# Token-major projections paired to 512 columns, two heads' products issued side by side, some weight splits made by GpSimd DMA

## The chip, the cores and the metric

The kernel runs on one NeuronCore of one Trainium2 chip. The metric is the device time of one execution in microseconds; it is given as the median of a few runs.

## The reference

Two decoder layers run over 256 tokens of width 1024 in float32. Each layer has a mixer with four groups of 256 columns and a convolutional FFN:

```python
proj = einsum('bsd,de->bse', rms_norm(x, norm_mix[i]), w_in[i])
qa, ka, va, qb, kb, vb, c_val, c_gate, qm = split(proj, 9 sections of 256)
o_a = moba_attention(rope(norm(qa)), rope(norm(ka)), va)       # 4 heads of 64, causal
o_b = dilated_attention(rope(norm(qb)), rope(norm(kb)), vb)    # 4 heads of 64, causal
o_c = silu(layer_norm(depthwise_conv31(c_val * sigmoid(c_gate)))) @ w_conv_out
km, vm = split(rms_norm(mem) @ w_mem_kv[i])                    # memory of 256 rows
o_m = softmax(norm(qm) @ norm(km).T * scale) @ vm              # 4 heads of 64, no mask
x = x + group_rms_norm(concat(o_a, o_b, o_c, o_m)) @ w_out[i]
gate, val = split(depthwise_conv3(rms_norm(x) @ w_up[i]))      # width 2 x 2816
x = x + (silu(gate) * val) @ w_down[i]
```

## The kernel before

**Split products.** Most products are made in fp32r, with both operands split into a high and a low part. An activation has the tiles `Hh` and `Hl`. A weight unit of 128x2048 floats (1 MB) is staged in an `st` slot by a DMA on SyncE's queue; ACT copies it, rounded, into a `wh` slot and DVE writes the difference `st - wh` into a `wl` slot, 1024 columns at a time (`get`, `split`). One product is then three matmuls: `wh` with `Hh`, `wl` with `Hh`, `wh` with `Hl`. There are 4 `st`, 3 `wh` and 3 `wl` slots, and `INORDER` makes them, and the two PSUM banks `pj`, be handed out in the order of the units. A few products are plain fp32: layer 0's first section (the gate `cg`, from the tile `whole`, which sits in an `st` slot) and the output products of groups 1 and 3 (`gy` with `st`).

**Sections.** A section is one of the nine 256-column parts of `w_in`, or `km` or `vm`; its unit holds all 8 chunks of 128 rows. The two convolution sections are channel-major (`proj`), the other nine token-major (`proj_tok`): the stationary operand is a 128-token block of `Hh` or `Hl`, the moving one 256 columns of `wh` or `wl`, so a section is 2 token blocks x 8 chunks x 3 = 48 matmuls of 256 columns. After it `head_norm` makes squares on ACT, head by head with an accumulator, then the rope and the scaling on DVE, four transposes on PE and a copy on ACT. `ORDER` gives the sections of a layer in the order of their units; the memory sections of layer 1 are made in layer 0's FFN.

**Attention.** For two chunks of two heads each, `attention` records per head: two score products (64 contraction rows, PSUM tag `sc`), softmax on DVE and ACT, transposes, and a copy; then per head two products with V (64 output rows, tile `o`). Three `sc` banks serve both scores and transposes.

**Order.** Nothing is issued directly: operations are recorded on logical tiles with an estimated duration, a list scheduler (`schedule`) picks for each engine the operation that can start first by these estimates, and `emit` issues the result. Each engine then runs its own list strictly in order and waits on semaphores. Issues of DMAs stand in SyncE's list in the same way.

Of the kernel before, what the change touches and what calls it, by code (L numbers as in the profile page):

```python
# [10 lines left out]
F32 = mybir.dt.float32  # L11
# [24 lines left out]
PASSES = ((1,0),(3,),(2,))  # L36
CO_AT = 1
# [28 lines left out]
def unit_order():  # L66
    names = []
    for l in range(DEPTH):
        for s in ORDER[l]:
            names += [(l, s)] if s != "mem" else [(l, "mem"), (l, "km"), (l, "vm")]  # L70
# [4 lines left out]
        for i in range(NPAIR):  # L75
            names.append((l, f"up{i}"))
            if i == MEM_AT and l + 1 < DEPTH:
                names += [(l + 1, "mem"), (l + 1, "km"), (l + 1, "vm")]
# [21 lines left out]
def pack_weights(i):  # L100
    parts = []
    for l, n in UNITS:
# [5 lines left out]
        elif n in ("km", "vm"):  # L108
            s = ("km", "vm").index(n)
            parts.append(kpack(i["w_mem_kv"][l][:, s * GW:(s + 1) * GW]))  # L110
# [83 lines left out]
class View:  # L194
# [21 lines left out]
    def heads(self):  # L216
        """[P, 2, 256] as [P, 2, heads, 64]"""
        a = self.idx.shape[0]
        return View(self.t, self.idx.reshape(a, 2, 4, HD), self.dtype, self.chain + (("heads", 0),))
# [18 lines left out]
    def real(self, phys):  # L238
# [3 lines left out]
        for what, arg in self.chain:  # L242
# [6 lines left out]
            elif what == "heads":  # L249
                ap = ap.rearrange("p b (h d) -> p b h d", h=4)  # L250
            elif what == "spread":
# [22 lines left out]
LAT_PE, LAT_X, LAT_TO_PE, LAT_SAME, LAT_DMA = 197.0, 140.0, 260.0, 127.0, 2000.0  # L274
HAM, COLD = 3413.0, 0.45
# [3 lines left out]
class Rec:  # L279
# [16 lines left out]
    def op(self, eng, meth, args, kw, reads, writes, dur, table=None, after=(), label=""):  # L296
# [9 lines left out]
        def dep(p, kind):  # L306
            if kind == "raw" or p.eng != eng:
                if p.eng == "dma":
                    lat = LAT_DMA
# [38 lines left out]
    def mm(self, out, lhsT, rhs, start, stop, label="mm"):  # L348
        n = rhs.shape[-1] if len(rhs.shape) == 2 else rhs.shape[1] * rhs.shape[2]
        if rhs.dtype == F32R:  # L350
            dur = n / 2.4 + 2.5
        else:
            dur = max(4 * (n / 2.4 + 1), 214.0)
            if lhsT.shape[-1] == 64:
# [3 lines left out]
                       dur, label=label)  # L358

# [49 lines left out]

    def recip(self, out, a):  # L410
        n = int(np.prod(out.shape[1:]))
        return self.op("dve", "reciprocal", (out, a), {}, [a], [out], n * 6.5 + 67)
# [104 lines left out]
    def late(self, blend):  # L517
        """keys from the latest starts that keep the end of the schedule"""
# [20 lines left out]
    def emit(self, tc, phys):  # L539
# [21 lines left out]
def inside(a, b):  # L561
# [600 lines left out]
```

## Time and profile before

| | before |
|---|---|
| median of 3 runs | 643.03 us (642.45 to 643.16) |
| span of the profiled execution | 641.4 us |
| PE, weight loads | 632.3 us (99%), 603.5 us (94%) |
| DVE, ACT, POOL | 508.6, 432.3, 1.1 us |

The profiled execution is known by its span, from the first to the last instruction; the median stands 1.6 us above it, and that is taken as what lies around the span. A matmul's duration in the profile includes the tail of its pipeline, so the spacing of starts, and not the duration, tells what one costs.

### The profile page before, as it was taken

To read this page: it belongs to the slowest core of one execution; us is meant where nothing else is said; L and a number is where in the kernel's file an instruction comes from. 1 tells how busy PE (TensorE), PEld (TensorE's weight loads), DVE (VectorE), ACT (ScalarE), POOL (GpSimd) and SP (SyncE) were. 2 spreads that over 40 slices of the span, in tenths; PEclk is the share of its full clock that TensorE was granted. 3 is DMA by queue.
4 is the path that set the end of the run, shared out by engine and by line. 5 is a ranking of instruction groups with operands and counts; after the bars stand their busy time and mean duration, and the time that the engine had idled before them with its cause. 6 is when DMAs were issued, how large, how long until landed. Compare 5 with 4: busy or idle time off the path is not lost.

```text
span 641.4 us, 12448 instructions
## 1 busy us (share of the span) xinstructions
PE 632.3 (99%) x4940; PEld 603.5 (94%) x4940; DVE 508.6 (79%) x956; ACT 432.3 (67%) x966; POOL 1.1 (0%) x9
## 2 busy tenths in 40 slices
PE   7999999999999999999999999999999999999997
PEld 5998887899999999999999998679999999999997
DVE  5898898779888677787779898958987787777773
ACT  6979987767687765555658888867765555555541
POOL 0000000000000000000000000000000000000000
PEclk9999999999999999999999999999999999999999
DMA  8961231745656555554454531036445554545301
GB/s 279 376 266 67 83 131 67 246 148 179 217 189 228 196 198 191 166 175 170 155 197 160 195 123 66 2 138 255 160 169 198 198 191 164 176 193 197 133 2 66
DMA packets 17627, 107.59 MB, mean 168 GB/s; under 512 B 2080, under 2 KB 2848, under 8 KB 5280
## 3 DMA queue, kind: packets, MB, share of 16 engines
q1 hardware_dynamic: 17568, 106.79, 46.9%
q8 instruction: 39, 0.64, 0.4%
q14 instruction: 20, 0.16, 0.1%
HBM read 105.73 MB, written 1.05 MB: 166 GB/s over the span
## 4 chain that ended last, share of the span: by engine, by line
PE 96%; DVE 1%; ACT 1%; DMA 1%; SPq 0%; issue 0%; ACTq 0%
PE pj L554 67%; PE sc L554 18%; PE o L554 8%; PE ss L554 3%; DMA X<-in_x 1%; SPq L554 0%; DVE sm L554 0%; DVE X L554 0%; ACT pr L554 0%; ACT wh L554 0%; DVE tt L554 0%; DVE pr L554 0%; ACT v L554 0%; ACT t L554 0%; ACT qn L554 0%
## 5 line engine op out<-in xcount | busy, mean ns | idle before, releaser
L554 DVE TENSOR_TENSOR wl<-st,wh 128x1024 fp32r<-128x1024 f32 (+1 forms) x186 | 217.5, 1200 | 9.1 <-ACT wh L554 8.9
L554 ACT ACTIVATE wh<-st 128x1024 fp32r<-128x1024 f32 (+1 forms) x186 | 189.8, 1040 | 39.2 <-PE pj L554 38.8
L554 PE MATMUL pj<-Hl,wh 128*128 128x256 f32 x752 | 213.0, 284 | 0.0
L554 PE MATMUL pj<-Hh,wl 128*128 128x256 f32 x752 | 212.8, 283 | 0.0
L554 PE MATMUL pj<-Hh,wh 128*128 128x256 f32 x752 | 212.6, 283 | 0.0
L554 PEld LDWEIGHTS pj<-Hh,wl 128*128 128x128 f32 x752 | 144.2, 192 | 0.1
L554 PEld LDWEIGHTS pj<-Hh,wh 128*128 128x128 f32 x752 | 144.1, 192 | 0.0
L554 PEld LDWEIGHTS pj<-Hl,wh 128*128 128x128 f32 x752 | 144.1, 192 | 0.1
L554 PE MATMUL pj<-wh,Hh 128*128 128x256 f32 x288 | 82.8, 288 | 0.1
L554 PE MATMUL pj<-wl,Hh 128*128 128x256 f32 x288 | 82.9, 288 | 0.0
L554 PE MATMUL pj<-wh,Hl 128*128 128x256 f32 x288 | 82.9, 288 | 0.0
L554 DVE TENSOR_TENSOR tr<-pj,rx 128x512 f32<-128x512 f32 x46 | 31.8, 691 | 61.9 <-PE pj L554 61.4
L554 DVE SCALAR_TENSOR_TENSOR tq<-tr,vec,tq 128x254 f32<-128x254 f32 (+1 forms) x176 | 75.1, 477 | 0.7 <-ACT tq L554 0.7
L554 PE MATMUL sc<-al,wh 128*128 128x256 f32 x264 | 74.4, 283 | 0.0
L554 PE MATMUL sc<-ah,wl 128*128 128x256 f32 x264 | 74.2, 282 | 0.0
L554 PE MATMUL sc<-ah,wh 128*128 128x256 f32 x264 | 73.3, 281 | 0.0
L554 ACT ACTIVATE tq<-tq 128x256 f32<-128x256 f32 x44 | 18.3, 416 | 77.5 <-DVE tq L554 77.4
L554 ACT ACTIVATE tq<-tr,vec 128x256 f32<-128x256 f32 x88 | 47.7, 589 | 13.1 <-DVE tr L554 13.1
L554 PEld LDWEIGHTS pj<-wl,Hh 128*128 128x128 f32 x288 | 55.1, 191 | 1.4 <-issue 1.2
L554 PEld LDWEIGHTS pj<-wh,Hh 128*128 128x128 f32 x288 | 55.1, 191 | 1.3 <-issue 0.8
L554 PEld LDWEIGHTS pj<-wh,Hl 128*128 128x128 f32 x288 | 55.1, 191 | 0.5 <-issue 0.5
L554 DVE SCALAR_TENSOR_TENSOR y<-upad,vec,y 128x256 f32<-128x256 f32 x120 | 51.3, 477 | 0.9 <-ACT y L554 0.7
(121 smaller groups left out, 982.7 us busy)
## 6 DMA issues: line engine op xcount, KB each, us to landing
st<-in_w SPq DMA_DIRECT2D x94, 1024.0 KB, 4.9
st<-in_w SPq DMA_DIRECT2D x9, 256.0 KB, 5.4
st<-in_mem SPq DMA_DIRECT2D x2, 1024.0 KB, 5.7
out_x<-X SPq DMA_DIRECT2D x4, 256.0 KB, 3.0
X<-in_x SPq DMA_DIRECT2D x3, 256.0 KB, 5.3
gb<-in_gain SPq DMA_DIRECT2D x2, 320.0 KB, 6.5
cst<-in_cst SPq DMA_DIRECT2D x1, 448.0 KB, 7.4
X<-in_x SPq DMA_DIRECT2D x2, 128.0 KB, 2.7
```

The source lines that it names most:

```text
L554: getattr(engs[o.eng], o.meth)(*[real(a) for a in o.args], **{k: real(v) for k, v in o.kw.items()})
```

## The change

- **Pairs.** qa with ka, qb with kb, va with vb, and km with vm become pairs. A pair's unit holds 4 chunks of rows of both sections side by side, so there are still two units of 1 MB for a pair, but each is needed for half of the chunks. `proj_pair` makes, for each token block, 8 chunks x 3 = 24 matmuls of 512 columns into a whole PSUM bank: 48 for a pair, where two sections had 96 of 256 columns. `head_norm` now works on one token block of a pair, with one square over 512 columns on ACT and a sum per head on DVE.
- **Heads.** `together` records the four score products of two heads as one operation, and `emit` issues them alternating between the heads; likewise the four products with V. The transposes of the probabilities go to the `ss` banks (3 now), and `sc` has 2.
- **GpSimd DMA.** For the units named in `SOFT`, a DMA on GpSimd's queue writes the rounded weights straight from memory into `wh`, ACT writes `-wh` into `wl`, and a second, accumulating DMA adds the weights to `wl`. `st` and DVE are not used. `SOFT` names ten units; `qka0` is staged ahead of time by other code and takes the old path, so nine units are made so, three in layer 0 and six in layer 1.
- **Order and slots.** Both `ORDER`s, `CO_AT` (where the convolution's output product stands) and the slots change: 3 `st`, 4 `wh`, fewer of some small tiles. Every one of FFN's products is as before.

```diff
+SOFT = (('qkb', 'qka'), ('qkb', 'vv', 'qm', 'wo0'))
-ORDER = ("cg qa va cv ka qb kb vb qm mem", "kb cv cg qb ka qa vb va qm")
+PAIRS = {"qka": ("qa", "ka"), "qkb": ("qb", "kb"), "vv": ("va", "vb"), "mem": ("km", "vm")}
+ORDER = ("cg cv qka vv qkb mem qm", "qka cg cv qkb vv qm")
-CO_AT = 1
+CO_AT = 2
...
+LAT_SOFT = 6000.0
...
+    def together(self, out, products, dur, label):
+        reads = [v for p in products for v in p[1:3]]
+        return self.op("pe", "together", tuple(products), {}, reads, out, dur, label=label)
...
+    def soft(self, out, src, add=False):
+        kw = dict(accum_op=ALU.add) if add else {}
+        return self.op("pool", "dma_start", (out, src), kw, [out] if add else [], [out], 1000.0)
...
+            if o.meth == "together":
+                for out, lhsT, rhs, start, stop in o.args:
+                    nc.tensor.matmul(real(out), real(lhsT), real(rhs), start=start, stop=stop, skip_group_check=True)
+                continue
...
-    "st": (4, UNIT, F32), "wh": (3, UNIT, F32R), "wl": (3, UNIT, F32R), "Hh": (2, NC * 256, F32R), "Hl": (2, NC * 256, F32R),
+    "st": (3, UNIT, F32), "wh": (4, UNIT, F32R), "wl": (3, UNIT, F32R), "Hh": (2, NC * 256, F32R), "Hl": (2, NC * 256, F32R),
...
-PSLOTS = {"pj": 2, "ss": 2, "sc": 3, "o": 1}
+PSLOTS = {"pj": 2, "ss": 3, "sc": 2, "o": 1}
...
+            self.r.key -= self.AHEAD
+            self.r.soft(hi[:, :cols], src)
+            for a in range(0, cols, 1024):
+                b = min(cols, a + 1024)
+                self.r.act(lo[:, a:b], hi[:, a:b].bitcast(F32), AF.Copy, scale=-1.0)
+            self.r.soft(lo[:, :cols], src, True)
...
+    def proj_pair(self, ws, H, name):
+        for m in range(2):
+            ps = self.bank("pj", f"{name}{m}")
+            flat = ps.flat()
+            for k in range(NC):
+                t = slice(m * P, (m + 1) * P)
+                w, c = ws[k // 4], slice(k % 4 * 512, (k % 4 + 1) * 512)
+                for a, b in ((0, 0), (0, 1), (1, 0)):
+                    self.r.mm(flat, H[a][:, k, t], w[b][:, c], k == 0 and a == b == 0, k == NC - 1 and a == 1, name)
+                self.r.key += 2 * T_MM3
+            yield m, ps
...
-        for b in range(2):
-            for h in range(4):
-                c = slice(h * HD, (h + 1) * HD)
-                r.act(junk[:, b, c], ps[:, b, c], AF.Square, accum_out=s8[:, 4 * b + h:4 * b + h + 1])
+        r.act(junk.heads(), q, AF.Square)
+        s8 = self.t("s8", [P, n, 4])
+        r.reduce_sum(s8, junk.heads())
...
+            r.together(scs, [(scs[hh][:, ofs[j]:ofs[j] + wid[j]], q[half[hh], c, j * P:(j + 1) * P],
+                              k[half[hh], c, :wid[j]], True, True) for j in range(2) for hh in range(2)],
+                       100.0 + sum(4 * w / 2.4 for w in wid), "sc")
...
+            r.together([o], [(o[half[hh], c, (slice(0, 256), cols)[j]], v[:, j, (2 * c + hh) * HD:(2 * c + hh + 1) * HD],
+                              pts[hh][:, (slice(0, 256), late)[j]], j == 0, j == 1) for j in range(2) for hh in range(2)],
+                       100.0 + 4 * (256 + (P if causal else 256)) / 2.4, "pv")
```

**PE, the first token-major unit of layer 0.** Before, the section qa (`wh_72`, `wl_75`) follows the gate of the convolution, one token block after the other for each chunk:

```order
L554 MATMUL pj_143<-wh_71,Hl_79 128x256
L554 MATMUL pj_142<-wh_72,Hh_77 128x256
L554 MATMUL pj_142<-wl_75,Hh_77 128x256
L554 MATMUL pj_142<-wh_72,Hl_79 128x256
L554 MATMUL pj_142<-wh_72,Hh_77 128x256
```

Now the pair qka follows the second convolution section. Its first chunks come from `qka0` (`wh_71`, `wl_75`); further on in the same pair the other half, `qka1` (`wh_72`, `wl_76`), takes over:

```order
L591 MATMUL pj_139<-Hh_77,wl_74 128x256
L591 MATMUL pj_138<-wh_71,Hh_77 128x512
L591 MATMUL pj_139<-wh_71,Hh_77 128x512
L591 MATMUL pj_138<-wl_75,Hh_77 128x512
L591 MATMUL pj_138<-wh_71,Hl_79 128x512
```

And 24 rows later, where the chunks of `qka1` begin:

```order
L591 MATMUL pj_139<-wl_75,Hh_77 128x512
L591 MATMUL pj_139<-wh_71,Hl_79 128x512
L591 MATMUL pj_139<-wh_72,Hh_77 128x512
L591 MATMUL pj_138<-wl_76,Hh_77 128x512
L591 MATMUL pj_138<-wh_72,Hl_79 128x512
L591 MATMUL pj_138<-wh_72,Hh_77 128x512
```

Each row is one matmul, now of 512 columns, and from chunk 4 on PE stands behind `wl_76`, which a GpSimd DMA completes.

**SyncE, the same place.** Before, the third unit (qa) goes into the fourth `st` slot, `st_70`, and the constants and gains follow it:

```order
L554 DMA vec_64<-in_vec 128x268 [waits DMAHW7_49]
L554 DMA st_70<-in_w 128x2048 [waits DMAHW0_49]
L554 DMA cst_62<-in_cst 128x896 [waits DMAHW1_49]
L554 DMA gb_94<-in_gain 128x640 [waits DMAHW2_49]
L554 DMA st_67<-in_w 128x2048 [waits DMAHW3_49,DVE_49,PE_49]
```

Now there is no fourth slot, and `qka0` goes into `st_67`, where the tile `whole` lies until PE has made the first section's products:

```order
L591 DMA vec_64<-in_vec 128x268 [waits DMAHW7_49]
L591 DMA st_67<-in_w 128x2048 [waits DMAHW0_49,DVE_49,PE_49]
L591 DMA cst_62<-in_cst 128x896 [waits DMAHW1_49]
L591 DMA qk_108<-in_gain 128x640 [waits DMAHW2_49]
L591 DMA st_68<-in_w 128x2048 [waits DMAHW3_49]
```

The unit's DMA, and the constants and gains behind it in this list, have moved behind a wait for PE and DVE.

**ACT, from the end of the first norm.** Before, ACT converts qa (`wh_72`) and then squares its result head by head:

```order
L554 ACT_TABLE_LOAD
L554 ACTIVATE tr_102<-tr_102 128x512 [waits DVE_49]
L554 ACTIVATE wh_72<-st_70 128x1024 [waits DMAHW0_49]
L554 ACTIVATE wh_72<-st_70 128x1024
L554 ACTIVATE ts_100,s_91<-pj_143 128x64 [waits PE_49]
L554 ACTIVATE ts_100,s_91<-pj_143 128x64 x7
```

Now it converts `qka0` (`wh_71`), and right behind it writes `-wh` of `qka1` into `wl_76`:

```order
L591 ACTIVATE tr_100<-tr_100 128x512 [waits DVE_49]
L591 ACTIVATE wh_71<-st_67 128x1024 [waits DMAHW0_49]
L591 ACTIVATE wh_71<-st_67 128x1024
L591 ACTIVATE wl_76<-wh_72 128x1024 [waits DMASW0_49]
L591 ACTIVATE wl_76<-wh_72 128x1024
L591 ACTIVATE wh_73<-st_68 128x1024 [waits DMAHW3_49,DMAHW2_49]
```

GpSimd's list, where the accumulating DMA of `qka1` is its second DMA, behind that copy on ACT:

```order
L591 MEMSET fill_63 128x128
L591 DMA wh_72<-in_w 128x2048
L591 DMA wl_76<-in_w 128x2048 [waits Activation_49]
L591 DMA wh_71<-in_w 128x2048 [waits DVE_49,PE_49]
L591 DMA wh_72<-in_w 128x2048 [waits DMASW0_49,PE_49]
L591 DMA wl_76<-in_w 128x2048 [waits DMASW1_49,Activation_49]
```

So the low part of a unit made in this way passes through three engines' lists: the first DMA, ACT in its turn, the second DMA.

## Rows read from the trace of the kernel before

**Rows 1.** The page of the kernel before: its span, part 1 (busy time of each engine, its share of the span, instructions), a row of part 2 (the GB/s that the DMA engines moved in 40 slices of 16 us), and part 4 (the chain of work that ended last: shares of the span by engine).

```profile
span 641.4 us, 12448 instructions
...
PE 632.3 (99%) x4940; PEld 603.5 (94%) x4940; DVE 508.6 (79%) x956; ACT 432.3 (67%) x966; POOL 1.1 (0%) x9
...
GB/s 279 376 266 67 83 131 67 246 148 179 217 189 228 196 198 191 166 175 170 155 197 160 195 123 66 2 138 255 160 169 198 198 191 164 176 193 197 133 2 66
...
PE 96%; DVE 1%; ACT 1%; DMA 1%; SPq 0%; issue 0%; ACTq 0%
```

**Rows 2.** Busy time by stretch of the span (start:end in us; length; then for PE, the weight loads PEld, DVE, ACT and POOL the busy us with the number of instructions; the granted TensorE clock as a share of 2.4 GHz; share of the DMA engines; GB/s). The first two rows are layer 0's attention, the third is layer 0's FFN, the last is attention in layer 1.

```profile
50.00:90.00 40.00, 39.70 (x298) 34.63 (x297) 35.34 (x105) 36.51 (x139) 0.00 (x0) 1.00 0.23 84
90.00:127.00 37.00, 36.50 (x205) 29.40 (x203) 31.09 (x66) 27.79 (x62) 0.00 (x0) 1.00 0.45 151
...
140.50:347.00 206.50, 206.50 (x1725) 206.50 (x1724) 163.93 (x273) 134.72 (x240) 0.00 (x0) 1.00 0.54 188
...
380.00:410.00 30.00, 29.35 (x205) 23.58 (x205) 26.84 (x88) 26.70 (x92) 0.00 (x0) 1.00 0.13 48
```

**Rows 3.** PE in order of time in the FFN, around 301 us (start, duration with its pipeline tail, instruction): products of 256 columns in the split fp32r form, one after the other. Every row in between is one such product too; from the first row shown to the last there are 15 intervals.

```profile
301.09 0.28 PE L554 MATMUL pj<-Hh,wh 128*128 128x256 f32 x1
...
302.89 0.28 PE L554 MATMUL pj<-Hh,wh 128*128 128x256 f32 x1
```

**Rows 4.** PE in order of time at the start (start, duration, instruction with its count, idle before it): fp32 products of layer 0's first section, which the profile records as two instructions each.

```profile
4.66 2.21 PE L554 MATMUL pj<-st,st 128*128 128x256 f32 x8
8.77 4.99 PE L554 MATMUL pj<-st,st 128*128 128x256 f32 x22 [1.90 <-DVE Hl L554]
13.59 0.59 PE L554 MATMUL ss<-ssum,fill 128*128 128x256 f32 x2
```

**Rows 5.** Groups of instructions by form (count | busy us, mean ns of one | idle before): the token-major section products, which are made three times each in this shape (wh with Hh, wl with Hh, wh with Hl), and the weight loads of the first kind.

```profile
L554 PE MATMUL pj<-wh,Hh 128*128 128x256 f32 x288 | 82.8, 288 | 0.1
...
L554 PEld LDWEIGHTS pj<-wh,Hh 128*128 128x128 f32 x288 | 55.1, 191 | 1.3 <-issue 0.8 <-ACT v L554 0.4
```

**Rows 6.** The chain of waits in the two attention stretches, in order of time (start, us, what and how many records): the products P*V, tile o. Four records are one head, eight are two heads next to each other. Up to 83 us they are layer 0's causal heads, around 101 to 110 and 417 to 426 the memory attention's, in between layer 1's causal ones.

```profile
55.77 0.80 PE o L554 x4
59.09 0.81 PE o L554 x8
...
101.28 1.01 PE o L554 x4
...
401.92 0.81 PE o L554 x8
...
404.50 0.86 PE o L554 x4
...
425.23 1.01 PE o L554 x4
```

**Rows 7.** The same chain: the scores, tile sc. Four records are one head, eight are two heads, twelve are three.

```profile
49.85 0.86 PE sc L554 x8
51.43 0.92 PE sc L554 x4
...
92.56 1.07 PE sc L554 x8
...
96.36 1.13 PE sc L554 x4
...
378.27 1.50 PE sc L554 x12
...
382.32 0.85 PE sc L554 x4
```

**Rows 8.** PE in order of time around 92 us (start, duration, instruction and count): scores of the memory attention and the product that follows them.

```profile
92.49 1.99 PE L554 MATMUL sc<-qn,qn 64*128 64x256 f32 x12
94.41 0.39 PE L554 MATMUL pj<-ah,wh 128*128 128x256 f32 x1
```

**Rows 9.** The chain of waits at the start of the program (start, us, what).

```profile
3.06 4.91 DMA X<-in_x
```

**Rows 10.** SyncE's DMA issues in order of time (start, us, what): a run of six weight units, of which the first is issued at 15.09.

```profile
15.09 15.69 SPq L554 DMA_DIRECT2D st<-in_w  x6
```

**Rows 11.** Part 6 of the page, DMA issues: the weight units (1 MB each; the last number is the median us from issue to landing).

```profile
st<-in_w SPq DMA_DIRECT2D x94, 1024.0 KB, 4.9
```

**Rows 12.** Groups of instructions by form: the weight splits on DVE and ACT, the squares of the head norm with the reads of their accumulators, and DVE's reduction of a 128x512 tile.

```profile
L554 DVE TENSOR_TENSOR wl<-st,wh 128x1024 fp32r<-128x1024 f32 x180 | 213.6, 1217 | 9.1 <-ACT wh L554 8.9
L554 ACT ACTIVATE wh<-st 128x1024 fp32r<-128x1024 f32 x180 | 186.3, 1054 | 39.2 <-PE pj L554 38.8
...
L554 ACT ACTIVATE ts<-pj 128x64 f32<-128x64 f32 x96 | 20.0, 239 | 2.8 <-PE pj L554 2.5
L554 ACT ACTIVATION_READ_ACCUMULATOR ts<-pj 128x1 f32 x96 | 19.6, 224 | 0.0
...
L554 DVE TENSOR_REDUCE sm<-sc 128x2 f32<-128x512 f32 x8 | 5.3, 683 | 0.2 <-PE sc L554 0.2
```

**Rows 13.** DVE (first row) and ACT (the other two) in order of time: the section's scaling, the conversion of one weight unit, and the first square of a head norm, which waits for the end of the second section's products.

```profile
16.07 0.68 DVE L554 TENSOR_TENSOR tr<-pj,rx 128x512 f32<-128x512 f32 x1
...
18.53 1.99 ACT L554 ACTIVATE wh<-st 128x1024 fp32r<-128x1024 f32 x2
20.85 0.22 ACT L554 ACTIVATE ts<-pj 128x64 f32<-128x64 f32 x1 [0.33 <-PE pj L554]
```

More of the change, by code (lines that the diff above doesn't have):

```diff
@@ L69, in unit_order @@
         for s in ORDER[l]:
-            names += [(l, s)] if s != "mem" else [(l, "mem"), (l, "km"), (l, "vm")]
+            names += [(l, s)] if s not in PAIRS or s == "mem" else []
+            names += [(l, f"{s}{j}") for j in range(2)] if s in PAIRS else []
         for i, gs in enumerate(PASSES):
@@ L107, in pack_weights @@
             parts.append(kpack(i["w_in"][l][:, s * GW:(s + 1) * GW]))
-        elif n in ("km", "vm"):
-            s = ("km", "vm").index(n)
-            parts.append(kpack(i["w_mem_kv"][l][:, s * GW:(s + 1) * GW]))
+        elif n[:-1] in PAIRS:
+            rows = slice(int(n[-1]) * D // 2, (int(n[-1]) + 1) * D // 2)
+            if n[:-1] == "mem":
+                parts.append(kpack(i["w_mem_kv"][l][rows]))
+            else:
+                two = [SECT.index(s) * GW for s in PAIRS[n[:-1]]]
+                parts.append(kpack(np.concatenate([i["w_in"][l][rows, c:c + GW] for c in two], axis=1)))
         elif n == "co":
@@ L216, in heads, with quads @@
     def heads(self):
-        a = self.idx.shape[0]
-        return View(self.t, self.idx.reshape(a, 2, 4, HD), self.dtype, self.chain + (("heads", 0),))
+        a, n = self.idx.shape[:2]
+        return View(self.t, self.idx.reshape(a, n, 4, HD), self.dtype, self.chain + (("heads", 0),))
+    def quads(self):
+        a, _, n = self.idx.shape
+        return View(self.t, self.idx.reshape(a, 2, 2, n), self.dtype, self.chain + (("quads", 0),))
     def spread(self, axis, n):
@@ L250, in real @@
                 ap = ap.rearrange("p b (h d) -> p b h d", h=4)
+            elif what == "quads":
+                ap = ap.rearrange("p (a b) n -> p a b n", a=2)
             elif what == "spread":
@@ L408, in reduce_max, with reduce_sum @@
                        [out], n * 1.04 + 69)
+    def reduce_sum(self, out, a):
+        n = int(np.prod(a.shape[1:]))
+        return self.op("dve", "tensor_reduce", (out, a), dict(axis=mybir.AxisListType.X, op=ALU.add), [a], [out],
+                       n * 1.04 + 69)
     def recip(self, out, a):
@@ L774, in head_norm @@
-        tp = self.bank("ss", f"t{name}")
-        for c in range(2):
-            for b in range(2):
-                r.transpose(tp[:, c, b * P:(b + 1) * P], n[:, b, c * P:(c + 1) * P], self.C("ident", P))
-        qn = self.t("qn", [P, 2, 256], name)
-        r.act(qn, tp, AF.Copy)
-        return (qn, s8) if tab is not None and len(tab) == 1 else qn
-    def v_tok(self, ps, st, name):
-        v = self.t("v", [P, 2, 256], name)
-        for j in range(2):
-            self.r.act(v[:, j, :], ps[:, j, :], AF.Copy, scale=st["rt"][:, j:j + 1])
-        return v
+            r.tt(x, x, t, ALU.add)
@@ L788, in attention, with query_m @@
+    def query_m(self, ps, st, name):
+        tp, s8 = self.head_norm(ps.heads(), [st["et"][:, b:b + 1] for b in range(2)], self.tabs[2],
+                                [((b, c), c) for c in range(2) for b in range(2)])
+        qn = self.t("qn", [P, 2, 256], name)
+        self.r.act(qn.flat(), tp.flat(), AF.Copy)
+        return qn, s8
     def attention(self, q, k, v, mask, name):
@@ L976, in mixer @@
                 whole = st.get("whole") if i == 0 else None
-                w = self.get(l, n, whole is None)
+                if n in PAIRS:
+                    got = self.pair(l, n, st)
+                    for key, x in zip(PAIRS[n], got):
+                        done[key] = x
+                    w = None
+                else:
+                    w = self.get(l, n, whole is None)
                 h = H if whole is None else whole
-                if n[0] == "c":
+                if w is None:
+                    pass
+                elif n[0] == "c":
                     done[n] = self.proj(w, h, n)
@@ L1005, in ffn @@
         H = st["H"]
-        acc = [self.bank("sc" if b < 3 else "o", f"acc{b}") for b in range(4)]
+        acc = [self.bank(("sc", "sc", "o", "ss")[b], f"acc{b}") for b in range(4)]
         pend, dn, ga = [], {}, {}
```

136 lines of the change are left out of this document (78 added, 58 removed).

## The prediction

> **What bounds the kernel now.** I read the page first, part 1 against part 4: PE is busy for 99% of the span and PE alone is 96% of the chain that ended last [rows 1]. So a microsecond taken from PE's own list is a microsecond of the span, as long as the other engines keep up, and a wait put into that list costs its full length. Second, the stretches: in the FFN both PE and its weight loads are busy all the time; in the attention stretches of both layers the weight loads leave 5 to 8 us of each 30 to 40 us idle, while DVE is busy 35.3 of 40 and ACT 36.5 of 40 us [rows 2]. There PE is still the longest chain, but with two engines close behind it. The granted clock is 1.00, that is 2.4 GHz, in every stretch [rows 2].
>
> Third, what a product costs. In the FFN 15 intervals between starts take 1.80 us, so a split product of 256 columns costs 0.120 us [rows 3]. An fp32 product of the same shape is recorded twice, and each record takes (13.59 - 8.77) / 22 = 0.219 us [rows 4]. Its time is nearly double for the same shape and one weight load per record; it is the nearest row to a product that streams 512 columns over one weight load.
>
> **Wide products.** Of the 3 x 288 token-major products [rows 5], 3 x 32 are qm's and stay; 768 become 384 of 512 columns. Before: 768 x 0.120 = 92.2 us. After, at 0.219: 84.1. **Saved 8.1 us.** The bounds: at the granted 2.4 GHz, 512 columns cannot take under 0.213 us, which would save 10.2; if columns themselves cost 0.120 per 256, a wide product takes 0.240 and nothing is saved. I take 0.219, because the fp32 records show a row in which PE goes faster per column than 256 in 0.120.
>
> On this the Trainium skill (TensorE: Matmul & The Clock Gate, Back-to-back issue gap) says that a product of N columns takes N/2.4 + 2.5 ns, 109 ns for 256 and 216 ns for 512. By that rule for both shapes the pairs would save only about 1.0 us, and the sum below would be 638.6. The trace contradicts it for the narrow shape, with 0.120, so I keep the rows.
>
> **Heads side by side.** One causal head's products with V take 0.80 us, two heads next to each other 0.81; the two halves of the array work at once [rows 6]. Before, 3 of 8 causal pairs stand together (the first at 59.09, the last at 401.92), 10 heads stand alone (55.77 to 404.50), and so do the 8 heads of the memory attention at 1.01 (101.28 to 425.23). Now all 12 pairs stand together: 5 x 0.80 + 4 x 1.01 = **8.0 us**. For the scores, two neighbouring heads take 0.86 (causal) or 1.07 (memory) [rows 7], as a pair will. A causal attention took 49.85 to 52.35, 2.50 us, in layer 0 and 1.50 + 0.85 in layer 1 [rows 7], against 2 x 0.86: 2 x 0.78 + 2 x 0.63 = 2.8. The memory attention took 92.49 to 94.41 and 1.13 [rows 7, 8], against 2 x 1.07: 0.9 each, 1.8 in two. **Saved 4.6 us** here, 12.6 together. The lower bound is 0, if PE's gaps fill with waits: a pair's V products wait for the slower head. ACT and DVE lose load as well: nine units less to split on DVE, 18 x 1.22 = 22 us, against 14 new reductions of at most 0.68; and each head norm's 8 squares and 8 reads, 3.3 us busy, become one pass [rows 12]. So I let them take back **3 us** of the 12.6, near the lower end of 0 to 12.6. That is a choice: both engines have some tenth of their time free in these stretches [rows 2].
>
> **The start.** Three things are added here.
>
> First, GpSimd's first DMA (1 MB) waits for nothing and lands in the time in which PE's chain waits 4.91 us for X [rows 9]. The DMA engines then moved 279 GB/s in the first slice and at most 376 [rows 1]. If that megabyte goes in front of the rest of X, it costs 1.05 MB / 376 = 2.8 us; if it comes behind, nothing. I take the middle, **1.4**, as packets of both queues may mix.
>
> Second, `qka0` has no free `st` slot. Its DMA goes out where the next run of units went out before, at 15.09 [rows 10], and lands 4.9 us later [rows 11], at 20.0. ACT's conversion takes 1.99 for both halves [rows 13], so the first half is there at 21.0. DVE has the scaling of the second section in front (0.68 as in [rows 13]), which waits for PE's end of that section at 20.5 [rows 13], then splits in 1.22: 22.4. PE fills 0.44 of that with two high products and waits **1.5**. Here the early slot of the kernel before was the cover.
>
> Third, `qka1`. ACT copies `-wh` behind `qka0`, from 22.0 to 24.0, and only then GpSimd may add. PE has 24 products of `qka0` and the first of `qka1` to make: 22.4 + 24 x 0.219 = 27.7. No row shows an accumulating DMA or one of GpSimd's. The lower bound is the 4.9 us of a plain unit [rows 11], the upper twice that, 9.8, because adding moves the target too. I take 7, between them, and the wait is 24.0 + 7 - 27.7 = **3.3** (1.2 to 6.1). Behind it in PE's list stands everything, vv above all; behind `-wh` on ACT stand the conversions of vv, which have until PE's end of qka.
>
> **The later GpSimd units.** For qkb in layer 0, the copy on ACT stands behind the square of qka's last block, so GpSimd adds about 3.4 us after PE has left qka (0.6 square, 0.2 for the scaling, 2.0 copy, and the wait for DVE's sum). PE then has vv (48 x 0.219 = 10.5) and one pair of scores (0.86): some 8 us of cover. In layer 1 the second half of vv needs the `wl` slot of qkb's first half; from its release PE has 12 + 13 + 10 products (7.7), scores and transposes (1.6), less ACT's 2.1: 7 us of cover. At 7 both just suffice, so these cost **0**, and each microsecond beyond costs one at the start, one in qkb from 8 on, and one in vv from 7 on. The other units of layer 1 (qkb, qm, `wo0`) have more.
>
> At no cost, as they lie off PE's list: fewer `st` slots in the FFN (three of them, a unit each 5.8 us by 48 x 0.120, and 4.9 for landing plus some 3 for conversion), nine megabytes more to read (9.4 of 107 MB, with the DMA engines 13 to 54% busy in these stretches after the start [rows 2]), and the reduced squares. Without that cover a late unit costs PE what it is late.
>
> **Sum.** 641.4 - 8.1 - 12.6 + 3.0 + 1.4 + 1.5 + 3.3 = 629.9 us of span. The median stood 1.6 above the span, so **631.5 us**.
>
> **Rivals.**
>
> *Late additions (slower).* If an accumulating DMA takes L, the start pays L - 7 more, qkb L - 8 and vv L - 7. At L = 11 that is 4 + 3 + 4 = 11 us and the time 642.5; from L = 11.6 on it is slower by over 0.2%; at 12 it is 645.5. For it speaks that the path runs through three in-order lists and that two DMAs may share the engines; against it, that 11.6 is beyond twice a plain unit. The Trainium skill (SBUF — State Buffer, Who interferes with whom) says that GpSimd can be locked out of the port it shares with VectorE while that engine runs certain operations, which starves the DMAs that GpSimd describes. As a mechanism here: one split on DVE lasts 1.22 us [rows 12], and a DMA that waits for one or two of these adds 1.2 to 2.4 to L, 3 to 6 us to the time, 634 to 638; no row of before shows it. It alone doesn't decide.
>
> *The wide product gains nothing.* At 0.240 the time is 631.5 + 8.1 = 639.6. For it: a stream of 256 columns ends at 2.13 columns per ns, and no row has a split product that is wider. Against: the fp32 records.
>
> *The heads' gain turns into waits.* All 12.6 come back: 641.1, at the edge of no change. For it: ACT's 36.5 of 40 us. Against: ACT's and DVE's load falls in the same stretches.
>
> *No wait for the additions.* With L = 4.9, the first megabyte behind X, 0.213 per wide product and nothing given back: 631.5 - 2.1 - 1.4 - 2.1 - 3.0 = 622.9.
>
> **Chances.** The forecast as summed, within 626 to 637: 0.58. No wait: 0.12. The wide product without gain: 0.08. The heads' gain lost: 0.07, half of it within 0.2% of before, which is about what a measurement of this kernel can tell from no change. Late additions with L from 11 on: 0.15, of which 0.02 lie below 11.6 and are no change, 0.13 slower. So faster 0.81, same 0.06, slower 0.13. The range leaves out the far end of the late additions and little below: 622 to 644.
>
> **What would show it.** Products of 512 columns with starts 0.22 us apart (0.24 would refute the first term). V products of two heads in about 0.8 us for all twelve pairs. In the first 35 us, PE waiting once for `qka0` (1 to 2 us) and once for a GpSimd DMA into `wl` (about 3 us), with X landing a little later than 7.97. PE's spacing of 0.120 in the FFN as before. The prediction is wrong if GpSimd's accumulating DMAs land more than 8 us after their issue, if PE waits for them in qkb or vv, or if DVE and ACT, and no longer PE, make most of the chain between 40 and 120 us.

## The result: 1.4% slower, and the profile after

The changed kernel takes 651.66 us (median, 650.86 to 654.13) against 643.06 us of the kernel before in the same session: ratio 1.014, 95% interval 1.0128 to 1.0152. The forecast was 631.5 us, with a range of 622 to 644; it missed. The profiled execution took 651.61 us.

From the page of the changed kernel, against [rows 1]: span, busy time, the granted TensorE clock in 40 slices of 16 us (tenths of full speed), the queue of GpSimd's DMAs, the shares of the chain of waits, and the DMA issues with the median us from issue to landing.

```profile
span 649.8 us, 11481 instructions
...
PE 623.8 (96%) x4556; PEld 578.4 (89%) x4556; DVE 498.3 (77%) x946; ACT 420.9 (65%) x780; POOL 14.0 (2%) x27
...
PEclk8969999999999999999999989999999999999999
...
q0 software_dynamic: 2592, 18.88, 11.5%
...
PE 85%; DMA 6%; issue 5%; DVE 3%; POOL 1%; ACT 1%; SPq 0%; POOLq 0%; ACTq 0%
...
st<-in_w SPq DMA_DIRECT2D x85, 1024.0 KB, 4.9
wh<-in_w POOLq DMA_DIRECT2D x9, 1024.0 KB, 6.5
wl<-in_w POOLq DMA_DIRECT2D x9, 1024.0 KB, 9.4
```

PE is busy 8.5 us less than before and the span is 8.4 us longer. PE was idle for 9.1 us before (641.4 - 632.3) and is for 26.0 now. And it no longer runs at full clock throughout. In the start, in order of time (start, duration, instruction, idle before it and who ended it):

```profile
30.63 0.39 PE L591 MATMUL pj<-wh,Hl 128*128 128x512 f32 x1
30.86 0.39 PE L591 MATMUL pj<-wh,Hh 128*128 128x512 f32 x1
39.24 0.77 PE L591 MATMUL pj<-wl,Hh 128*128 128x512 f32 x1 [8.00 <-ACT sqc L591]
39.80 0.63 PE L591 MATMUL pj<-wh,Hl 128*128 128x512 f32 x1
```

POOL's issue of the DMA that this product waits for:

```profile
26.90 0.87 POOL L591 DMA_DIRECT2D wl<-in_w  x1 [24.61 <-ACT wl L591]
```

And the same stretch in windows (columns as in [rows 2]: PE, PEld, DVE, ACT and POOL busy, granted clock, DMA share, GB/s):

```profile
25.00:30.00 5.00, 4.53 (x20) 3.72 (x21) 3.85 (x9) 2.91 (x4) 0.87 (x1) 1.00 1.02 421
30.00:35.00 5.00, 1.25 (x6) 0.71 (x4) 5.00 (x6) 3.57 (x5) 0.56 (x1) 0.87 1.04 244
35.00:40.00 5.00, 0.76 (x2) 0.70 (x3) 1.66 (x5) 1.81 (x6) 0.00 (x0) 0.50 1.00 329
40.00:45.00 5.00, 5.00 (x16) 3.95 (x15) 3.58 (x11) 3.63 (x11) 0.00 (x0) 0.61 0.99 403
```

And the DMAs of 1 MB that were issued from 18 to 46 us (how many, KB, median us from issue to landing), in the changed kernel and then in the kernel before:

```profile
st<-in_w SPq DMA_DIRECT2D x5, 1024.0 KB, 11.0
...
wl<-in_w POOLq DMA_DIRECT2D x1, 1024.0 KB, 12.2
wh<-in_w POOLq DMA_DIRECT2D x1, 1024.0 KB, 12.8
```

```profile
st<-in_w SPq DMA_DIRECT2D x5, 1024.0 KB, 5.6
```

Two things are to be seen. First, `qka1`'s accumulating DMA is issued at 26.90, lands 12.2 us later, at 39.1, and PE goes on at 39.24. (The profile names ACT as the releaser here. The landing decides, and in the run with 15 taps below the same wait of 7.93 us is put down to the DMA into `wl`.) It was not slow alone: with all DMA engines busy, five loads of units by SyncE had a median of 11.0 us in this stretch, where the kernel before needed 5.6. Second, when PE comes back the granted clock is half (1.2 GHz), where [rows 2] showed 1.00 in every stretch, and products of 512 columns start 0.43 us apart and not 0.23 as at 30.63 and 30.86. In layer 1 two more accumulating DMAs are late:

```profile
374.32 0.47 PE L591 MATMUL pj<-wl,Hh 128*128 128x512 f32 x1 [3.96 <-DMA wl<-in_w]
...
392.05 0.47 PE L591 MATMUL pj<-wl,Hh 128*128 128x512 f32 x1 [1.80 <-DMA wl<-in_w]
```

### The profile page after: what moved, and what is told of

Same layout as the page of the kernel before. It is cut to its first block, busy times and chain, and to the rows that moved or that the text cites. A ratio compares the mean times of both kernels' runs of the same rounds, so it can differ in the third digit from the quotient of the medians.

```text
span 649.8 us, 11481 instructions
## 1 busy us (share of the span) xinstructions
PE 623.8 (96%) x4556; PEld 578.4 (89%) x4556; DVE 498.3 (77%) x946; ACT 420.9 (65%) x780; POOL 14.0 (2%) x27
## 4 chain that ended last, share of the span: by engine, by line
PE 85%; DMA 6%; issue 5%; DVE 3%; POOL 1%; ACT 1%; SPq 0%; POOLq 0%; ACTq 0%
PE pj L591 59%; PE sc L591 10%; PE ss L591 8%; PE o L591 5%; DMA wl<-in_w 3%; DMA st<-in_mem 2%; PE o L589 1%; PE sc L589 1%; DMA X<-in_x 1%; DVE y L591 1%; DVE wl L591 0%; POOL wl L591 0%; POOL wh L591 0%; DVE tt L591 0%; DVE gy L591 0%
## 5 line engine op out<-in xcount | busy, mean ns | idle before, releaser
L591 ACT ACTIVATE wh<-st 128x1024 fp32r<-128x1024 f32 (+1 forms) x168 | 170.2, 1037 | 70.5 <-PE pj L591 52.5
L591 PE MATMUL pj<-wl,Hh 128*128 128x512 f32 (+1 forms) x160 | 62.4, 390 | 14.5 <-ACT sqc L591 8.0
L591 PE MATMUL pj<-wh,Hh 128*128 128x512 f32 (+1 forms) x160 | 61.4, 387 | 0.5 <-ACT wh L591 0.2
L591 PE MATMUL pj<-wh,Hl 128*128 128x512 f32 (+1 forms) x160 | 61.4, 387 | 0.0
L591 PEld LDWEIGHTS pj<-wl,Hh 128*128 128x128 f32 x160 | 31.1, 194 | 22.1 <-ACT sqc L591 8.4
L591 PE MATMUL sc<-ah,wl 128*128 128x256 f32 x176 | 49.7, 283 | 0.0
L591 PE MATMUL sc<-al,wh 128*128 128x256 f32 x176 | 49.7, 283 | 0.0
L591 PE MATMUL sc<-ah,wh 128*128 128x256 f32 x176 | 49.1, 281 | 0.0
L591 PEld LDWEIGHTS pj<-wh,Hh 128*128 128x128 f32 x160 | 30.9, 193 | 7.0 <-issue 1.1
L591 PEld LDWEIGHTS pj<-wh,Hl 128*128 128x128 f32 x160 | 31.3, 196 | 5.3 <-issue 0.3
```

## Three sums for every run

Every span is taken apart in the same way. *Idle* is span less PE's busy time. *Half clock* is what PE lost while it worked: in windows of 2 us, PE's busy time times (1 - granted clock), summed. *Work* is the rest, what PE's list would take without a wait at full clock. Times are medians; the sums are of the one profiled execution. t4 and w2 are the same program, and their sums differ by 0.6 (idle), 3.1 (half clock) and 1.0 us (work), so a difference of that size between two rows need not come from their kernels. In u4, v4 and w1 the work holds added products of zeros, some 14.7, 7.5 and 8.2 us.

| run | time | span | idle | half clock | work |
|---|---|---|---|---|---|
| before | 643.06 | 641.4 | 9.1 | 0.0 | 632.3 |
| changed | 651.66 | 649.8 | 26.0 | 5.6 | 618.2 |
| s1 no GpSimd DMA | 652.74 | 649.5 | 24.1 | 5.7 | 619.7 |
| s2 in layer 1 only | 657.35 | 653.3 | 29.2 | 3.7 | 620.4 |
| s3 in layer 0 only | 650.19 | 648.4 | 23.8 | 6.8 | 617.8 |
| s4 all but `qka1` | 648.30 | 646.0 | 24.3 | 3.2 | 618.5 |
| t4 layer 0's qkb only | 644.12 | 642.5 | 17.1 | 6.3 | 619.1 |
| t1 heads in turn undone | 651.91 | 649.8 | 27.1 | 4.9 | 617.8 |
| t2 halves of 256 | 655.42 | 654.3 | 26.5 | 6.7 | 621.1 |
| t3 before, with heads | 646.37 | 644.7 | 20.0 | 3.3 | 621.4 |
| u1 t4, heads apart | 663.29 | 662.1 | 17.0 | 6.7 | 638.4 |
| u2 t4, four `st` | 652.72 | 650.5 | 23.0 | 10.5 | 617.0 |
| u3 both | 665.16 | 660.6 | 21.4 | 5.5 | 633.7 |
| u4 changed, 66 zeros | 660.35 | 658.8 | 20.6 | 5.0 | 633.2 |
| v1 before, 15 taps | 644.27 | 643.1 | 10.0 | 1.7 | 631.4 |
| v2 t3, 15 taps | 643.05 | 642.7 | 15.8 | 4.6 | 622.3 |
| v3 changed, 15 taps | 659.29 | 656.3 | 31.4 | 6.6 | 618.3 |
| v4 changed, 33 zeros | 654.10 | 652.9 | 20.9 | 7.5 | 624.5 |
| w1 t4 with zeros | 641.77 | 640.5 | 13.6 | 0.0 | 626.9 |
| w2 t4 again | 643.94 | 641.0 | 17.7 | 3.2 | 620.1 |

So the change did take 14.1 us of work from PE (632.3 to 618.2). It gave back 16.9 us of idle time and 5.6 of half clock.

## Experiments

**1. GpSimd's DMAs.** The only edit is the table:

```diff
-SOFT = (('qkb', 'qka'), ('qkb', 'vv', 'qm', 'wo0'))
+SOFT = ((), ())                                   # s1
+SOFT = ((), ('qkb', 'vv', 'qm', 'wo0'))           # s2
+SOFT = (('qkb', 'qka'), ())                       # s3
+SOFT = (('qkb',), ('qkb', 'vv', 'qm', 'wo0'))     # s4
+SOFT = (('qkb',), ())                             # t4
```

> The changed kernel with no unit made by GpSimd DMA: all go through st, ACT and DVE; pairs, heads, order and slots stay. Theory A (the accumulating DMAs land too late): the waits of 8.0 us for qka1 in layer 0, of 4.1 and 2.2 us in layer 1 go, and with them 2.3 and 1.9 us at half clock, 18.5 us in all: about 633 us. Rival B (the order and the three st slots: a pair needs two units at once, by whatever path): PE waits about as long at the same places, 648 us or more.

> GpSimd DMA in layer 1 only. Theory A: the 8.0 us wait for qka1 and the 2.3 us at half clock behind it go, layer 1's 8.2 us stay: about 641 us. Rival B: 648 us or more, as the start has the same demand for bytes by another path.

> GpSimd DMA in layer 0 only. Theory A: layer 1's waits of 4.1 and 2.2 us and 1.9 us of half clock go, the start's stay: about 643 us. Rival B: 650 us.

> One unit changed, qka1 of layer 0, which goes through st, ACT and DVE; the other eight stay with GpSimd. Theory A: it alone holds PE up at the start, so 10.3 us go: about 641 us, as with GpSimd DMA in layer 1 only. Rival (the start is bound by the bytes that all DMA engines together bring, 20 to 45 us): qka1's plain DMA lands late too, PE waits at about 31 us for over 4 us, 647 us or more.

> GpSimd DMA for the two qkb units of layer 0 alone. If the stages add up, it has the first mixer of the run with qka1 by st (134.7 us to the FFN), and the second mixer of the run without any GpSimd DMA (110.7 us): the last product at 636.4 us, a time of about 643.5 us, as the kernel before. If one of them depends on the other (order, slots), 646 us or more.

Theory A falls as the whole cause: without any GpSimd DMA (s1) the kernel takes 652.74 us, 1.0154 of before (1.0132 to 1.0175). The waits at 31, 370 and 390 us are gone, but others stand in their place. So Rival B, which had PE wait as long at the same places, is right on the time and wrong on the places. PE's waits in s1 (us in total, times, longest):

```profile
PE pj L591 <- DVE wl L591: 3.7, 2, 3.1
PE pj L591 <- DVE gy L591: 3.5, 4, 1.7
PE ss L591 <- ACT pr L591: 3.1, 4, 1.8
PE ss L591 <- DVE tq L591: 2.3, 1, 2.3
```

The largest end at 87.67 and 91.17 us. PE in order of time, and then DVE in the same stretch of s1:

```profile
87.67 0.44 PE L591 MATMUL ss<-cst,tq 128*128 128x128 f32 x2 [2.29 <-DVE tq L591]
91.17 0.58 PE L591 MATMUL pj<-wl,Hh 128*128 128x256 f32 x1 [3.07 <-DVE wl L591]
```

```profile
82.13 3.63 DVE L591 SCALAR_TENSOR_TENSOR y<-upad,vec,y 128x256 f32<-128x256 f32 x9
85.69 0.41 DVE L591 TENSOR_REDUCE s<-ts 128x4 f32<-128x256 f32 x1
86.01 1.26 DVE L591 SCALAR_TENSOR_TENSOR y<-upad,vec,y 128x256 f32<-128x256 f32 x3
87.20 0.41 DVE L591 TENSOR_TENSOR tq<-pj,s 128x256 f32<-128x256 f32 x1
87.53 2.45 DVE L591 SCALAR_TENSOR_TENSOR y<-upad,vec,y 128x256 f32<-128x256 f32 x6
89.91 1.21 DVE L591 TENSOR_TENSOR wl<-st,wh 128x1024 fp32r<-128x1024 f32 x1
```

DVE works without a pause, on taps of the convolution (`y`), while PE waits for a head norm (`tq`) and a split (`wl`) that stand behind them in its list: from 80 to 110 us DVE is busy 27.3 of 30 us and PE only 22.4, where PE had 29.9 before. That the taps cost s1 this time is read from the order of DVE's list; no run took the taps out of s1. GpSimd's DMAs spare DVE such splits; they are worth something where they land in time. By the runs: for layer 0's qkb -8.6 us (s1 to t4), for `qka1` +6.1 (t4 to s3) or +3.4 (s4 to changed), for the six units of layer 1 +4.6 (s1 to s2), +1.5 (s3 to changed) or +4.2 (t4 to s4). s4's misses (641 expected, 648.30 measured) and s2's show that the waits are not simply additive; t4 came out at 644.12, where the stages of the others had been added to 643.5.

Why `qka1` is late: in s4, with `qka1` loaded through `st`, PE has no wait over 1.3 us between 20 and 45 us. Loads are slow there too (9 to 11 us for the two units issued right behind `qka0`), but `qka1`'s single DMA goes out at about 16 us and not at 26.90, and so it lands in time. Two things added up, then: the addition was issued late, behind cast and copy, and it took 12.2 us, because other loads (mem, vv, the first of qkb) kept all DMA engines busy. The Trainium skill (DMA: Bandwidth & Descriptors, Issuing engines are not separate DMA queues) says that DMAs of all issuing engines run on the same 16 DMA engines and interleave. The trace agrees: in that stretch SyncE's units took 11.0 us (median) and GpSimd's 12.2 and 12.8. A lock that holds up GpSimd's DMAs alone, which the prediction weighed, is not needed to explain this, since SyncE's were nearly as slow.

**2. The two PE parts undone, and one of them alone.**

```diff
-  ... for j in range(2) for hh in range(2)]     # t1: inside one operation, both lists
+  ... for hh in range(2) for j in range(2)]
...
+            if o.meth == "matmul" and o.label in PAIRS and o.args[2].dtype == F32R:   # t2, in emit
+                for n in range(2):       # out and rhs cut to 256 columns each
```

t3 is the kernel before, whose `attention` records the scores and the V products of two heads with `together` as in the change; the transposes stay in its three `sc` banks.

> The changed kernel with one thing undone: inside each recorded operation the four products of the two heads are issued head by head again and not in turn; every other instruction keeps its place. Theory P (PE's own work sets the time of the mixers): 8 to 12.6 us come back, 660 to 664 us. Theory W (the vector and scalar chains and the weights set it; what PE saved it waits for elsewhere): under 4 us, 652 to 655 us.

> The changed kernel with each 512-column product issued as two of 256 columns, in the same place. 384 products at 0.229 us against 768 at 0.120: Theory P: 4.4 us more, 656 us. Theory W: within 1.5 us of the changed kernel, since those products stand where PE waits for weights anyway.

> The kernel before with the heads' part alone: the scores and the V products of two heads issued in turn; its units, order of sections, slots and DMAs stay. Theory P: 12.6 us less, about 631 us. Theory W: the softmax chains of DVE and ACT become what PE waits for, less than half of it remains: 637 to 643 us.

t1: no difference (651.91). It doesn't test the heads' gain after all, because the trace shows the same pairs: a V pair in the chain of waits of the changed kernel, and then of t1 (start, us, what and how many records):

```profile
68.65 0.80 PE o L589 x8
```

```profile
68.73 0.81 PE o L589 x8
```

Eight records take 0.80 us in either order; what counts is that two heads stand next to each other, as at 59.09 in [rows 6].

t2: 3.8 us slower by the medians, 2.9 by the work in the table; Theory P had 4.4, Theory W at most 1.5. Products of 256 columns stand 0.120 us apart there, of 512 in the changed kernel 0.228 (30.63 and 30.86 above).

t3 is the plainest of all runs. PE's work falls by 10.9 us, its idle time rises by 10.9, half clock adds 3.3, and the time is 3.2 us longer (1.0032 to 1.0062). PE's waits in it:

```profile
PE pj L563 <- ACT ah L563: 5.0, 2, 3.0
PE pj L563 <- DMA st<-in_w: 2.9, 1, 2.9
PE pj L563 <- DVE gy L563: 2.5, 3, 1.9
PE ss L563 <- ACT ts L563: 1.9, 2, 1.1
```

They stand at the ends of the two mixers (from 122 to 127 and from 402 to 413 us), and the one for a load at the start. For scores PE waits 0.3 us in all, so nothing here shows that pairs tie up the score banks.

**3. On t4: heads apart, and before's slots.** u1 records each head's products as operations of their own; u2 has 4 `st` and 3 `wh` for 3 and 4; u3 has both.

> The run with GpSimd DMA for layer 0's qkb alone (644.1 us), with the heads' part undone in the recording: each head's score products and V products are operations of their own again, which the scheduler places one by one. Theory W with a tie (recording two heads as one makes each wait for the later of them and takes two score banks at a time, and what PE saves is waited out): as fast or up to 3 us faster, 641 to 644.5 us. Theory P (PE's work counts): 8 to 12.6 us more, 652 to 657 us.

> The run with GpSimd DMA for layer 0's qkb alone, with the slots of the kernel before for the weights: 4 st and 3 wh for 3 st and 4 wh. If the three st slots hold up the loads where nearly all units go through st (PE waited 7.3 us for a load at 433 us in that run's chain): 2 to 5 us less, 639 to 642 us. If a fourth wh slot was worth as much: 643 to 645 us.

> Both edits of the two runs before this one. If their effects add up: 637 to 642 us, and then faster than the kernel before; if both only move the waits: 643 to 645 us.

All three (663.29, 652.72 and 665.16 us) are slower than any of these expectations. In u1 PE's work is 19.3 us more than in t4, with the same idle time, and the time is 19.2 longer: on the new order the heads' part is worth all of its PE time, and more than on the kernel before, where some heads stood together already [rows 6]. u2 changes no product and its work is the same within 2.1 us, yet it has 5.9 more idle and 4.2 more at half clock, and it costs 8.6 us. PE's list is in another order than in t4. Whether the `wh` slot that it lacks or this order costs the time, no run separates: none has four `st` and four `wh`.

**4. Is it VectorE's load?** The three runs leave out 16 of the 31 taps of the convolution, so part of the computation is missing.

```diff
-        for j in range(TAPS - 1, -1, -1):
+        for j in range(TAPS - 1, TAPS // 2, -1):
```

> The kernel before with 16 of the 31 taps of the convolution left out of each layer's mixer (so part of the computation is missing): 32 of 62 vector operations of 0.40 us a layer, 12.8 us of VectorE's time a layer, and nothing of PE's. It is the base for the two runs beside it. PE's products take the chain of the kernel before almost whole, so both theories expect little: 638 to 643 us.

> The kernel before with the heads' part alone, with the same 16 taps left out. Theory D (the heads' gain of 12.6 us on PE exists and is waited out behind VectorE's list, where the taps stand between the softmax steps): with the taps gone most of it shows, 8 us or more under the run beside it, some 626 to 632 us. Rival (recording two heads as one operation costs by itself, in score banks and in waiting for the later head): at or above that run, at most 4 us under it.

> The changed kernel with the same 16 taps left out. Theory D: what its mixers lose behind VectorE goes too, while the waits for the accumulating DMAs stay (about 10 us at the start, 6 in layer 1): 638 to 644 us, 8 to 14 us under the changed kernel. Rival (the waits for weights and the half clock are all of its loss): 648 us or more.

Before with 15 taps 644.27 us, with heads as well 643.05, changed 659.29. DVE's busy time fell by 24 us in each (508.6 to 485.0 and 509.2 to 485.5; 498.3 to 474.8), and no time fell by more than 3.3: v1 is even 1.3 us slower than the kernel before (638 to 643 was expected), v3 7.6 us slower than the changed one. Theory D falls as stated: with half of the taps gone the heads' part brings 1.2 us, at the edge of what can be measured, and not 8. v2 has 9.1 us less of PE's work than v1 (622.3 against 631.4) and only that much less time: its idle time is 5.8 more and its half clock 2.9 more. v3 has 31.4 us idle. In it the wait for `qka1` is named as what it is; POOL's issue and then PE:

```profile
25.45 0.87 POOL L591 DMA_DIRECT2D wl<-in_w  x1 [23.15 <-ACT wl L591]
```

```profile
37.70 0.77 PE L591 MATMUL pj<-wl,Hh 128*128 128x512 f32 x1 [7.93 <-DMA wl<-in_w]
```

What v2 does show is the end of a mixer, PE in order of time:

```profile
111.37 1.03 PE L563 MATMUL ss<-ts,fill 128*128 128x256 f32 x4
114.33 1.13 PE L563 MATMUL ss<-ts,fill 128*128 128x256 f32 x4 [1.93 <-ACT t L563]
116.92 10.19 PE L563 MATMUL pj<-gy,st 128*128 128x256 f32 x32 [1.47 <-DVE gy L563]
```

Two norms follow each other over PE, ACT and DVE with nothing left to put between; PE idles, the clock falls, and 32 fp32 records take 10.2 us, where at 0.219 [rows 4] they take 7.0.

**5. Is the half clock a price of its own?** In a first pair of runs, products of zeros (128x128, fp32) were put on PE in front of the product that waits for `qka1` at 31 us, 66 and then 33; they add exact zeros to the bank.

```diff
+            if o.meth == "matmul" and not filled and any(v.t.name == "wl0qka1" for v in o.args[1:]):
+                filled = True
+                for _ in range(33):          # u4: 66
+                    nc.tensor.matmul(real(o.args[0][:, :P]), real(zero), real(ident), start=False, stop=False,
+                                     skip_group_check=True)
```

> The changed kernel with 66 products of zeros (128x128, fp32, about 7 us by the 0.107 us that such a record takes here) added on PE in front of the first product that waits for qka1's accumulating DMA in layer 0, from 31 to 39 us; they add exact zeros to the bank. Nothing else moves. Theory C (half clock after a long wait is a price of its own): the clock stays at full over 39 to 45 us, the products there are 0.229 us apart and not 0.43, and some 2.3 us go: 649.3 us. Rival (what follows waits for vector and scalar work or for the next weights anyway): the clock stays up but the time does not move by more than 0.8 us, 651 to 652.5 us.

> As the run with 66 products of zeros, with 33, because each made two records of 0.111 us in that trace and all took 14.7 us, 6.9 us longer than the wait. 33 take about 7.3 us and end before the accumulating DMA lands. Theory C: full clock over 39 to 45 us, products there 0.229 us apart, 1 to 2.3 us less than the changed kernel: 649.3 to 650.6 us. Rival: the clock stays up, the time does not move: 651 to 652.5 us.

u4 (660.35) was mis-sized: its 132 records took 14.7 us. In v4 they end before the DMA lands, and the clock stays up:

```profile
32.23 7.53 PE L594 MATMUL pj<-cst 128*128 128x128 f32 x66
40.59 0.47 PE L596 MATMUL pj<-wl,Hh 128*128 128x512 f32 x1 [0.83 <-ACT Hh L596]
40.90 0.40 PE L596 MATMUL pj<-wh,Hl 128*128 128x512 f32 x1
```

From that product to the first product of the FFN v4 takes 98.3 us (40.59 to 138.87), the changed kernel 100.2 (39.24 to 139.46): 1.9 us had back, of 2.3 expected. The time doesn't show it: 654.1 us (651.11 to 654.64), as v4's start was 1.2 us later and its second mixer 3.6 us longer, though it is the same list. In the profiled execution v4 lost more to half clock than the changed kernel, 7.5 us against 5.6: what it kept behind `qka1` it lost at the start and in layer 1, where the clock was half for longer. Such kernels vary by 3 us or more from one execution to the next (s2 by 6), where the kernel before varies by 1. So the second pair ran on t4, which has waits but fewer GpSimd DMAs, in five rounds: 37 products of zeros in front of seven instructions, given by their place in PE's list.

```diff
+FILL = {176: 12, 2504: 3, 2506: 2, 2508: 3, 2511: 6, 2519: 2, 2522: 9}
...
+                for _ in range(FILL.get(npe, 0)):
+                    nc.tensor.matmul(real(out), real(zero[:, :out.shape[0]]), real(ident[:, :out.shape[1]]), start=start, stop=start,
+                                     skip_group_check=True)
```

> The run with GpSimd DMA for layer 0's qkb alone (profiled span 642.5 us, 17.1 us of PE idle and 6.3 us lost to half clock while PE worked), with 37 products of zeros (128x128, fp32, 0.22 us each) in front of seven instructions at which PE waited there: 12 before the first product with qkb0's wl, 25 in layer 1 between 396 and 410 us. Nothing else moves. Theory C (the half clock behind a wait is a price of its own): most of the 6.3 us go, 638 to 641 us, faster than the kernel before. Rival (the products of zeros end in the way of the work, or what follows waits for other engines anyway): 643 us or more.

> The run with GpSimd DMA for layer 0's qkb alone once more, with no product added, as the base on the same chip: 644 us.

w1 takes 641.77 us (641.03 to 642.48), w2 643.94 (641.25 to 646.24), the kernel before 643.00. Against before w1 is 0.9981 (0.9973 to 0.999), and w2 1.0017 (1.0004 to 1.0029). The stretch of layer 1's attention, w1 and then w2:

```profile
400.00:408.00 8.00, 7.04 (x60) 5.89 (x60) 7.67 (x19) 6.11 (x20) 0.00 (x0) 1.00 0.12 35
408.00:416.00 8.00, 8.00 (x58) 6.43 (x57) 8.00 (x23) 6.71 (x20) 0.00 (x0) 1.00 0.00 0
```

```profile
400.00:408.00 8.00, 6.42 (x35) 3.76 (x35) 7.36 (x17) 5.82 (x19) 0.00 (x0) 0.79 0.14 33
408.00:416.00 8.00, 6.27 (x43) 4.87 (x43) 8.00 (x22) 6.68 (x18) 0.00 (x0) 1.00 0.01 2
```

Theory C holds, at a lower price than it said: 2.2 us of the 3 to 6 hoped for, between the ranges of the two expectations. In w1 nothing is lost to half clock any more, in w2 3.2 us are. The twelve executions of w2 go the same way without any edit, though there a longer wait may be behind both: those with a mean clock of 0.986 took 645.74 and 646.24 us, the one with 0.997 641.25. w1 is the only version here that beats both kernels, by 1.2 us against before, which is at the edge of what can be measured. The Trainium skill (TensorE: Matmul & The Clock Gate, HAM oscillation — how this bites in real kernels) tells of products that wait for DMAs, lose the clock and start their next group at half speed, at a price of half the throttled time. The trace agrees on the mechanism, while the price is lower: up to PE's last product the changed kernel's clock is half for 17.1 us, half of which would be 8.5, but PE is idle in a part of them and loses 5.6.

## Why the prediction was wrong, step by step

- **What bounds the kernel.** "A microsecond taken from PE's own list is a microsecond of the span, as long as the other engines keep up" is the step that failed; the condition was priced at 3 us. A 99% busy PE [rows 1] showed that the old order hid every other chain behind PE's work, not how long those chains are. t3 shows it with the heads' part alone: 10.9 us less work, 10.9 more idle, 3.3 at half clock. It is not that PE's time never counts: on the new order it does, 19.2 us of time for 19.3 of work in u1 and 3.8 for 2.9 in t2.
- **Wide products.** Mis-sized: 0.229 us each, not 0.219; 384 x (0.240 - 0.229) = 4.2 us saved, not 8.1. t2 measured 3.8 by its time and 2.9 by its work. The fp32 records were the wrong neighbour; the value lies inside the bounds given, about halfway to the rival "gains nothing".
- **Heads side by side.** Nearly right on PE: where they stand in the chain, two causal heads take 0.80 to 0.82 us with V and 0.86 for scores, two of the memory attention 1.01 and 1.06, and t3 saves 10.9 us of work for the 12.6 forecast. Wrong in the give-back of 3.0: t3 gave back 14.2 (10.9 idle, 3.3 half clock). The rival "the heads' gain turns into waits" had a chance of 0.07.
- **GpSimd's first megabyte** (1.4): mis-sized. The first section ended at 16.34, 2.75 us later than in [rows 4]: PE had made only 4 records before its wait for X, not 8, and then 26 records took 7.63 us (0.29 each, 0.219 in [rows 4]), with a granted clock of 0.68 from 10 to 15 us. In s4, where `qka1` isn't loaded so, the section ends at 13.51.
- **`qka0`** (1.5): right, 0.4 us of wait at 23.80 and 1.2 at 25.47, after a start that was later by those 2.75.
- **`qka1`** (3.3): the addition took 12.2 us, not 7, and PE waited 8.2. This is the rival "Late additions", whose rule (L - 7 more) gives 3.3 + 5.2 = 8.5. It was called unlikely because 11.6 is "beyond twice a plain unit"; twice a plain unit was an assumption with no row behind it. That other loads would be as slow at the same time (11.0 us for a plain unit) had no place in the sum.
- **The later units** (0): qkb in layer 0 waits 0.3 us, in layer 1 qkb waits 4.1 and vv 2.2, behind additions that took 11.2 and 10.4 us. With all the measured waits for additions in place of its own the sum would be about 643.0, still 8.7 us short.
- **The half clock** (5.6) stood in no term and in no rival.
- **Its own signs.** Two of the three signs of being wrong came true: all nine additions landed more than 8 us after their issue (9.0 to 12.2), and PE waited for them in qkb and vv. The third did not: PE and not DVE or ACT makes most of the chain from 40 to 120 us.

The whole: -14.1 of work where the terms said -20.7, +16.9 idle where they said +9.2 with the give-back, and +5.6. But no single term undone brings the forecast back. Without the late DMAs the time is the same (s1), and the eight runs that keep pairs and pairwise heads (changed, s1 to s4, t1, t4, u2) lie between 644 and 657 us with 617 to 620 us of work. What stays open is which waits another order could avoid: the scheduler plans with estimated times, and each edit that it saw, even one that only takes work away (v3), gave a list whose idle time differs, from 17.1 us (t4) to 31.4 (v3). That is shown; whether wrong estimates are to blame, and which, was not tested.

## What to carry to other kernels

On a kernel whose order hides everything behind one busy engine, price an edit to that engine by the waits that come out from behind it, and measure one such edit alone first: here (t3) 10.9 us of saved work came back as 10.9 us of idle time. A wait of some microseconds on TensorE can cost more than its length, since the products behind it may run at 1.2 GHz; a few products of zeros in the wait bought back 2.2 us. A chain of DMA, copy and accumulating DMA needs its landing time measured, among the loads that will run beside it, before it is put in front of a busy engine.

## What the runs showed of the hardware that was not expected

- An accumulating 1 MB DMA of GpSimd's landed a median 9.4 us after its issue, 12.2 us in the busy start; one that only rounds 6.5, a plain one of SyncE's 4.9. These medians mix quiet and busy stretches: from 18 to 46 us plain ones took 11.0 too. The addition at 398.43, which had another one beside it for its first 1.1 us only, took 9.0, and the DMA engines were fully busy for 184 GB/s:

```profile
400.00:404.00 4.00, 4.00 (x37) 3.22 (x36) 3.65 (x16) 3.94 (x15) 0.00 (x0) 1.00 1.06 184
```

- POOL's issue took 0.87 us for an addition and 0.55 for a DMA that only rounds.
- Split products of 512 columns stand 0.228 to 0.229 us apart, two of 256 columns 0.240.
- Two heads' fp32 products work at once in whatever order they are issued, so long as they are neighbours (0.80 and 0.81 us for eight records, as long as four of one head alone [rows 6]).
- The granted clock was 0.50 behind PE's wait of 8.2 us, and in w2 it fell to 0.79 over 400 to 408 us, behind waits of 0.3 to 0.9 us that followed each other. In the kernel before, whose longest wait was 1.9 us [rows 4], it was 1.00 in every stretch [rows 2]; a wait of 2.1 us at the same place (8.71 us) in the changed kernel was followed by 0.68 from 10 to 15 us.
